# Row sums: a partial sum handed on as an element of the next piece, and SyncE's wait on ScalarE moved into a no-op

## The chip, the cores and the metric

One core of one Trainium2 chip. The metric is the device time of one execution in microseconds. It is some 1.8 us longer than the span that the profile shows (162.37 against 160.6 for the profiled execution of the kernel before).

## The reference

```python
def setup_inputs():
    batch, seq, dim = 32, 512, 1024
    return {"x": np.random.randn(batch, seq, dim).astype(np.float32)}

def reference(x):
    return np.sum(x, axis=-1).astype(np.float32)
```

64 MiB are read, 64 KiB written. There are 16384 rows of 1024 values. Each of the 128 partitions gets 112 rows of a first block and 16 rows of a last one.

## The kernel before

The first seven large tiles are loaded through three buffers and summed by VectorE; ScalarE helps with the seventh. The last tile comes in ever smaller loads: 9, 4 and 2 rows, then the last row in two pieces of 544 and 480 columns. A row that comes late is summed by a custom instruction of VectorE, which adds one half of its columns to the other half and accumulates. Its accumulator can start from a constant or from a value per partition (`scalar`).

```python
    def pairs_dve(xt, a, b, first, acc, pairs):
        h = (a + b) // 2
        nc.vector.tensor_tensor_reduce(
            out=pairs[:, 0 : h - a], in0=xt[:, a:h], in1=xt[:, h:b], scale=1.0, scalar=first,
            op0=ADD, op1=ADD, accum_out=acc,
        )
# ... (the large tiles)
    last = 15 * D
    for i, k in ((0, CUT), (CUT, D)):          # CUT = 544
        nc.sync.dma_start(
            out=xt[:, last + i : last + k],
            in_=x_b[:, c * D + last + i : c * D + last + k],
        )
# ... (rows 0 to 12 of the last 16)
    pairs_dve(xt, 13 * D, 14 * D, 0.0, res[:, c + 13 : c + 14], pairs[2])
    rows_act(xt, res, 14, 1, c + 14)           # ScalarE
    pairs_dve(xt, last, last + CUT, 0.0, part, pairs[0])
    nc.vector.tensor_copy(out=seen, in_=part)
    pairs_dve(xt, last + CUT, last + D, part, res[:, c + 15 : c + 16], pairs[1])
    nc.sync.dma_start(out=out_b, in_=res)      # the store of the last block
```

The copy to `seen` has no use for its value. It carries VectorE's wait for `part`, so that the last sum itself has to wait for its load alone.

## Time and profile before

| | before |
|---|---|
| time, median of the first three runs | 162.13 us (162.09 to 162.22) |
| span of the profiled execution | 160.6 us |
| last load's landing to the end of the span | 2.79 us |
| last custom sum | 467 ns for 240 columns |
| VectorE's end to the start of the store | 64 ns |

The landing is the time at which the last of a transfer's sixteen semaphore updates arrives. The lines themselves stand in the prediction below. In a timeline line the two numbers are start and duration in us; then come engine (SPq is SyncE's queue), source line, operation, and output and input tiles with their sizes. In a group line the number before the last bar is the mean duration of one instruction in ns.

### The profile page before, as it was taken

What the parts mean: (1) busy time and instruction counts of PE and PEld (TensorE: products, weight loads), DVE (VectorE), ACT (ScalarE), POOL (GpSimd) and SP (SyncE); (2) the same over time, 40 slices, a digit from 0 to 9 for tenths busy, and PEclk for the clock granted to TensorE, in tenths of its full rate; (3) what the DMA queues carried; (4) which work ended last, traced back from release to release, by engine and by line L of the source; (5) the groups of instructions that cost most, each with busy time, mean ns of one, the idle gap of its engine ahead of it and who ended that gap; (6) DMA issues with size and microseconds to landing.
All of it is one profiled execution on the core that took longest, in us unless ns stands there. A gap on an engine that the chain in (4) does not pass through costs nothing.

```text
span 160.6 us, 120 instructions
## 1 busy us (share of the span) xinstructions
DVE 121.4 (76%) x16; ACT 17.2 (11%) x31; POOL 0.2 (0%) x4
## 2 busy tenths in 40 slices
DVE  0000059997799958999499994999949999598884
ACT  0000000000000000000000000000000000596892
POOL 0000000000000000000000000000000000000000
DMA  9997996996996996996996979979969969998991
GB/s 375 490 398 337 490 522 294 490 522 261 522 506 278 522 506 278 522 506 278 522 506 278 522 326 457 522 310 473 522 294 490 522 261 522 432 432 369 410 402 62
DMA packets 2169, 67.18 MB, mean 418 GB/s; under 512 B 505, under 2 KB 633, under 8 KB 889
## 3 DMA queue, kind: packets, MB, share of 16 engines
q1 hardware_dynamic: 2016, 67.12, 97.2%
q10 hardware_dynamic: 153, 0.06, 0.1%
HBM read 67.11 MB, written 0.07 MB: 418 GB/s over the span
## 4 chain that ended last, share of the span: by engine, by line
DMA 75%; DVE 22%; SPq 0%; issue 0%; DVEq 0%
DMA xt<-in_x_dram 75%; DVE res L43 21%; DVE pairs L59 1%; SPq L97 0%; DVE seen L114 0%; DVE part L59 0%; DVEq L122 0%; DVE res L59 0%
## 5 line engine op out<-in xcount | busy, mean ns | idle before, releaser
L43 DVE TENSOR_REDUCE res<-xt 128x16 f32<-128x16384 f32 (+3 forms) x9 | 119.8, 13309 | 36.6 <-DMA xt<-in_x_dram 36.6
L51 ACT ACT_TABLE_LOAD x1 | 1.3, 1283 | 138.3 <-DMA xt<-in_x_dram 138.3
L51 ACT ACTIVATE xt<-xt 128x1024 f32<-128x1024 f32 x15 | 15.6, 1042 | 2.2 <-DMA xt<-in_x_dram 2.2
L51 ACT ACTIVATION_READ_ACCUMULATOR xt<-xt 128x1 f32 x15 | 2.8, 186 | 0.0
L59 DVE CUSTOM_DVE_ANT_0 pairs<-xt 128x512 f32<-128x512 f32 (+1 forms) x2 | 1.1, 566 | 0.3 <-DMA xt<-in_x_dram 0.3
L59 DVE CUSTOM_DVE_ANT_0 pairs<-xt,part 128x240 f32<-128x240 f32 x1 | 0.5, 467 | 0.0
L114 DVE COPY seen<-part 128x1 f32<-128x1 f32 x1 | 0.2, 153 | 0.0
L59 DVE DVE_READ_ACCUMULATOR2_ANT res<- 128x1 f32 x2 | 0.2, 81 | 0.0
L159 POOL MEMSET const-bfloat16-1.0<- 128x1 bf16 x1 | 0.1, 101 | 0.0
L159 POOL MEMSET const-uint8-127<- 128x1 uint8 x1 | 0.1, 101 | 0.0
L159 POOL MEMSET const-float32-0.0<- 128x1 f32 x1 | 0.1, 98 | 0.2 <-issue 0.2
L159 POOL MEMSET const-float32-1.0<- 128x1 f32 x1 | 0.1, 98 | 0.0
L59 DVE DVE_READ_ACCUMULATOR2_ANT part<- 128x1 f32 x1 | 0.1, 84 | 0.0
## 6 DMA issues: line engine op xcount, KB each, us to landing
xt<-in_x_dram SPq DMA_DIRECT2D x1, 7680.0 KB
xt<-in_x_dram SPq DMA_DIRECT2D x1, 4608.0 KB, 32.4
xt<-in_x_dram SPq DMA_DIRECT2D x1, 2048.0 KB, 36.9
xt<-in_x_dram SPq DMA_DIRECT2D x1, 1024.0 KB, 39.0
xt<-in_x_dram SPq DMA_DIRECT2D x1, 512.0 KB, 3.9
xt<-in_x_dram SPq DMA_DIRECT2D x1, 272.0 KB, 39.1
xt<-in_x_dram SPq DMA_DIRECT2D x1, 240.0 KB, 38.9
xt<-in_x_dram SPq DMA_DIRECT2D x6, 40.9
```

The costliest lines, as they stand in the source:

```text
L43: nc.vector.tensor_reduce(out=res[:, c : c + n], in_=xt[:, j * D : (j + n) * D].rearrange("p (j d) -> p j d", d=D), axis=X, op=ADD,)
L51: nc.scalar.activation(out=v, in_=v, func=COPY, accum_out=acc)
L59: nc.vector.tensor_tensor_reduce(out=pairs[:, 0 : h - a], in0=xt[:, a:h], in1=xt[:, h:b], scale=1.0, scalar=first, op0=ADD, op1=ADD, accum ...
L114: nc.vector.tensor_copy(out=seen, in_=part)
L159: nc = _bacc.Bacc("TRN2", target_bir_lowering=False, num_devices=1)
```

## The change

Its intent is to shorten what stands behind the last load. The sum of the first piece is written into the column just ahead of the second piece's columns, with a zero beside it. The last sum then takes it as an element and needs no operand per partition. And SyncE's wait for ScalarE, which is over early, goes into a no-op, so that the store's own instruction is left with the wait for VectorE, which is over last.

```diff
-    part = rpool.tile([P, 1], F32, name="part")
-    seen = rpool.tile([P, 1], F32, name="seen")
+    tail = rpool.tile([P, D + 16], F32, name="tail")
+    part = tail[:, CUT + 14 : CUT + 15]
+    nc.vector.memset(tail[:, CUT + 15 : CUT + 16], 0.0)
+    seen = rpool.tile([P, 2], F32, name="seen")
 ... (ScalarE's instructions are kept in the list by_act; pairs_dve loses its argument `first`)
-    for i, k in ((0, CUT), (CUT, D)):
+    for i, k, gap in ((0, CUT, 0), (CUT, D, 16)):
         nc.sync.dma_start(
-            out=xt[:, last + i : last + k],
+            out=tail[:, i + gap : k + gap],
 ...
-    pairs_dve(xt, last, last + CUT, 0.0, part, pairs[0])
+    pairs_dve(tail, 0, CUT, part, pairs[0])
-    nc.vector.tensor_copy(out=seen, in_=part)
-    pairs_dve(xt, last + CUT, last + D, part, res[:, c + 15 : c + 16], pairs[1])
-    nc.sync.dma_start(out=out_b, in_=res)
+    nc.vector.tensor_copy(out=seen, in_=tail[:, CUT + 14 : CUT + 16])
+    pairs_dve(tail, CUT + 14, D + 16, res[:, c + 15 : c + 16], pairs[1])
+    tc.keep_in_program_order(nc.sync.keepalive_nop([nc.sync.lower_ap(res[:, c + 14 : c + 15])]))
+    store = nc.sync.dma_start(out=out_b, in_=res)
+    for i in by_act:
+        tc.declare_no_dep(store.ins, i.ins, reason="the wait is in the nop before it")
```

More of the change, by code (lines that the diff above doesn't have):

```diff
@@ L50, in sum_act, with pairs_dve @@
     def sum_act(v, acc):
-        nc.scalar.activation(out=v, in_=v, func=COPY, accum_out=acc)
+        return nc.scalar.activation(out=v, in_=v, func=COPY, accum_out=acc)
+    by_act = []
     def rows_act(xt, res, j, n, c):
         for i in range(n):
-            sum_act(xt[:, (j + i) * D : (j + i + 1) * D], res[:, c + i : c + i + 1])
-    def pairs_dve(xt, a, b, first, acc, pairs):
+            by_act.append(
+                sum_act(xt[:, (j + i) * D : (j + i + 1) * D], res[:, c + i : c + i + 1])
+            )
+    def pairs_dve(v, a, b, acc, pairs):
         h = (a + b) // 2
         nc.vector.tensor_tensor_reduce(
-            out=pairs[:, 0 : h - a], in0=xt[:, a:h], in1=xt[:, h:b], scale=1.0, scalar=first,
+            out=pairs[:, 0 : h - a], in0=v[:, a:h], in1=v[:, h:b], scale=1.0, scalar=0.0,
             op0=ADD, op1=ADD, accum_out=acc,
@@ L98, in row_sums @@
     last = 15 * D
-    for i, k in ((0, CUT), (CUT, D)):
+    for i, k, gap in ((0, CUT, 0), (CUT, D, 16)):
         nc.sync.dma_start(
-            out=xt[:, last + i : last + k],
+            out=tail[:, i + gap : k + gap],
             in_=x_b[:, c * D + last + i : c * D + last + k],
         )
+    by_act.clear()
     for i, k in zip(cuts[:2], cuts[1:3]):
@@ L108, in row_sums @@
         rows_act(xt, res, i + h, k - i - h, c + i + h)
-    pairs_dve(xt, 13 * D, 14 * D, 0.0, res[:, c + 13 : c + 14], pairs[2])
+    pairs_dve(xt, 13 * D, 14 * D, res[:, c + 13 : c + 14], pairs[2])
     rows_act(xt, res, 14, 1, c + 14)
-    pairs_dve(xt, last, last + CUT, 0.0, part, pairs[0])
-    nc.vector.tensor_copy(out=seen, in_=part)
-    pairs_dve(xt, last + CUT, last + D, part, res[:, c + 15 : c + 16], pairs[1])
-    nc.sync.dma_start(out=out_b, in_=res)
+    pairs_dve(tail, 0, CUT, part, pairs[0])
[5 more added lines that the diff above has]
+        tc.declare_no_dep(store.ins, i.ins, reason="the wait is in the nop before it")
 def kernel(tc: tile.TileContext, x: bass.AP, out: bass.AP):
```

## The prediction

> **What bounds the kernel now.** I read the page first, for what kind of limit there is. The row of DMA shares and the chain that ended last say that almost the whole span is the input stream:
>
> ```profile
> span 160.6 us, 120 instructions
> DMA  9997996996996996996996979979969969998991
> ## 4 chain that ended last, share of the span: by engine, by line
> DMA 75%; DVE 22%; SPq 0%; issue 0%; DVEq 0%
> HBM read 67.11 MB, written 0.07 MB: 418 GB/s over the span
> ```
>
> The stream is not touched by the change, so the question is only what stands between the last load and the end. For that I read the timeline of the last microseconds, then the waits and durations by source line.
>
> Timeline of the kernel before, last part (start, duration, engine, line, operation, output and input):
>
> ```profile
> 156.62 0.69 DVE L59 CUSTOM_DVE_ANT_0 pairs<-xt 128x512 f32<-128x512 f32 x1 [0.26 <-DMA xt<-in_x_dram]
> ...
> 157.24 0.44 DVE L59 CUSTOM_DVE_ANT_0 pairs<-xt 128x272 f32<-128x272 f32 x1
> 157.59 0.19 ACT L51 ACTIVATION_READ_ACCUMULATOR xt<-xt 128x1 f32 x1
> 157.61 0.08 DVE L59 DVE_READ_ACCUMULATOR2_ANT part<- 128x1 f32 x1
> 157.73 0.15 DVE L114 COPY seen<-part 128x1 f32<-128x1 f32 x1
> 157.82 0.47 DVE L59 CUSTOM_DVE_ANT_0 pairs<-xt,part 128x240 f32<-128x240 f32 x1
> 158.22 0.08 DVE L59 DVE_READ_ACCUMULATOR2_ANT res<- 128x1 f32 x1
> 158.36 0.35 SPq L116 DMA_DIRECT2D out_dram<-res  x1
> ```
>
> The reader should see two things. ScalarE's last sum ends at 157.59 + 0.19 = 157.78, half a microsecond before VectorE's at 158.22 + 0.08 = 158.30, so VectorE releases the store. And the last custom sum, with 240 columns, takes 0.47 us, longer than the 0.44 us of the one with 272 columns.
>
> The groups kept apart by shape give these durations to the nanosecond (the number before the last bar):
>
> ```profile
> L59 DVE CUSTOM_DVE_ANT_0 pairs<-xt 128x512 f32<-128x512 f32 x1 | 0.7, 692 | 0.3 <-DMA xt<-in_x_dram 0.3
> L59 DVE CUSTOM_DVE_ANT_0 pairs<-xt,part 128x240 f32<-128x240 f32 x1 | 0.5, 467 | 0.0
> L59 DVE CUSTOM_DVE_ANT_0 pairs<-xt 128x272 f32<-128x272 f32 x1 | 0.4, 441 | 0.0
> L114 DVE COPY seen<-part 128x1 f32<-128x1 f32 x1 | 0.2, 153 | 0.0
> ```
>
> The source lines of the two pieces' loads and of the store show when the last load lands, and a wait on SyncE that stands alone in front of the store:
>
> ```profile
> L100 SPq DMA_DIRECT2D xt<-in_x_dram x2: 328/382/437, 118.1 to 118.9; - x2
> ...
> DMA to landing us min/median/max: 38.9/39.0/39.1
> ...
> L116 SPq EVENT_SEMAPHORE  x1: 20068/20068/20068, 138.3 to 138.3; - x1
> L116 SPq DMA_DIRECT2D out_dram<-res x1: 347/347/347, 158.4 to 158.4; - x1
> ```
>
> The last load is issued at 118.9 and lands 38.9 us later, near 157.8: exactly where the last custom sum starts (157.82). So two things end together there: the copy, and the landing of the last piece. Everything after 157.82 is serial: custom sum, accumulator read, SyncE's wait, store, its landing 1.4 us later, closing barrier.
>
> To price the separate wait I looked at a transfer whose own instruction holds the wait on VectorE, the reload of a large tile:
>
> ```profile
> 99.55 17.22 DVE L43 TENSOR_REDUCE res<-xt 128x16 f32<-128x16384 f32 x1 [2.24 <-DMA xt<-in_x_dram]
> 116.80 0.33 SPq L97 DMA_DIRECT2D xt<-in_x_dram  x1
> ```
>
> VectorE ends at 116.77 and the transfer starts at 116.80, 0.03 us later. The store starts 158.36 - 158.30 = 0.06 us after VectorE.
>
> **What the Trainium skill says.** "VectorE: DVE Perf Modes", section "The TRN2 errata", gives (N+151)/0.96 ns for an fp32 add of two tensors. That is 691 for N = 512 and 441 for 272; this trace has 692 and 441 for the custom sums, so the formula carries over. For 240 it gives 407, and the trace has 467. The section "Scalar operands" of the same page describes the [P, 1] operand read per partition and names no cost for it; the trace's 60 ns is what I take.
>
> The same page, section "The DRAIN you can't avoid", says that a value just written is not safe to read by the next VectorE instruction without a semaphore or one instruction between. That is why the copy to `seen` remains in both kernels: no saving there. This case's traces can't show the hazard itself.
>
> "Perfetto Trace Analysis", section "Identifying Dependency Chains", says that an instruction waiting on several engines may get EventSemaphore instructions ahead of it with the additional conditions. The trace agrees: the 20.07 us EVENT_SEMAPHORE of the store's line is that instruction.
>
> **The change part by part.**
>
> 1. The pointer operand goes. The last custom sum of before starts from `part` as a per-partition scalar. After, `part` and a zero stand in the two columns ahead of the second piece; 482 columns are summed as two halves of 241. Duration by the formula: (241+151)/0.96 = 408 ns; by the slope of the two groups, (692-441)/(512-272) = 1.046 ns per column, 441 - 31 x 1.046 = 409. Take 408. Saving: 467 - 408 = 59 ns. The extra column costs about 1 of these. It lies wholly on the path, since the sum starts with the landing and nothing runs beside it that ends later. One caution: the pointer's cost could stand ahead of the recorded start. But the first 512-column sum too starts with its load's landing, and has no pointer; the landing of the last piece and the start of the sum stand equally close. So I put the cost inside the 467.
>
> 2. The order of waits on SyncE changes. The built program of before has an EventSemaphore that waits for VectorE (and an old transfer), then the store, which itself waits for ScalarE. ScalarE has long been done, so VectorE's end must first release the EventSemaphore, and only then is the store taken up: 0.06 us. After, an EventSemaphore for ScalarE comes first (the no-op), then one for the old transfer, and the store itself waits for VectorE. ScalarE's end at 157.78 leaves half a microsecond for the two, while the ones in a row at the end of the trace take 17 to 28 ns each. The store should then start 0.03 us after VectorE, as the reload does. From the timeline's rounding the saving is 0.06 - 0.03 = 0.03 us; the duration of the wait (from 138.27, 20.068 us, thus to 158.334, and the store about 0.03 later) puts it at 35 ns. Take 35.
>
> 3. A memset of one column is added on VectorE at the start. VectorE is idle until 22.08 us there: 0.
>
> 4. The copy reads two columns instead of one: 1 ns at most, hidden or nearly so behind the landing of the last piece.
>
> 5. The two last loads go to a tile of their own, with a 64-byte gap between them. Same sizes, same order, same queue, the same single wait: 0.
>
> 6. At the very end SyncE waits for the no-op's own semaphore as well as the others. The built program has as many EventSemaphores there as before: 0.
>
> Sum: 59 + 35 = 94 ns, at most 1 or 2 ns given back. 162.13 - 0.094 = 162.04 us.
>
> **The rivals.**
>
> The landing hides it. If the sum's start were what the change made earlier, the last load would eat the gain; the tie at 157.8 says so. But both savings are after that start, so the tie protects nothing. It would matter only for item 4. Had I overlooked something and all were hidden: 162.13.
>
> The read through the stream costs as much as through the pointer. The sum now takes an element that was written some 0.2 us earlier, by an accumulator read; a stall of the stream would show as 441 or more instead of 408. Nothing in the trace shows such a stall: `seen`, the copy that reads `part` directly behind its writer, takes only 153 ns. Then only the 35 ns would stay: 162.10.
>
> The no-op gets in the way: were SyncE to take each EventSemaphore late, after VectorE's end, two would stand in the path instead of one, and the store would start about 0.09 us after VectorE rather than 0.03: 162.13 - 0.06 + 0.03 = 162.10. Against it: half a microsecond between the two engines' ends.
>
> The pieces' new addresses change the landing. It is the one thing that could move the time by more than a tenth, in either direction, as the landing sets the start of the last sum. Against it: same packets, and the three runs of before lie within 0.13 us, which bounds what the stream does from run to run. I allow it 0.1 us.
>
> **Range and chances.** The center is 162.04. The runs of before spread by 0.13 us (162.09 to 162.22), so a median of a few has perhaps 0.04 of its own; the rivals with half the gain stand at 162.10, the one with none at 162.13. I take 161.92 to 162.16 for 8 in 10. Two per cent would be 3.2 us, more than everything behind the last landing (160.6 - 157.8 = 2.8 us in the profile), so "within 2%" is next to certain: 0.99, and 0.005 for each of the others.
>
> **What would show it.** Right: the last custom sum, 241 columns, with about 408 ns; the store's start 0.03 us after the end of VectorE's last accumulator read; the two EVENT_SEMAPHOREs of SyncE over before VectorE ends; from the start of the last sum to the end of the span 94 ns less than the 160.6 - 157.82 = 2.77 us of before. Item 1 is wrong if that sum takes 440 or more; item 2 if the store's gap stays at 0.06. If both are right and the time is still 162.13 or more, the landing of the last load has moved, or the store's 1.4 us has; its row and the last sum's start tell which. The prediction is wrong as a whole if the time leaves the range with the landing where it was.

## The result, and the profile after

| | before | after |
|---|---|---|
| time, median of six runs | 162.13 us (162.09 to 162.22) | 162.13 us (161.97 to 162.25) |
| span of the profiled execution | 160.6 us | 160.4 us |
| last load's landing to the end of the span | 2.79 us | 2.71 us |

The ratio is 0.9999, with a 95% interval of 0.9986 to 1.0012. A ratio here is the mean time of one kernel's runs over that of the other's of the same rounds, so it is not quite the ratio of the medians quoted. The interval is 0.26% wide, some 0.4 us: it can hold the predicted 0.09 us as well as nothing.

The chain of the page is as before:

```profile
span 160.4 us, 122 instructions
DMA 75%; DVE 22%; SPq 0%; issue 0%; DVEq 0%
```

The timeline's end, in the changed kernel:

```profile
157.48 0.19 ACT L55 ACTIVATION_READ_ACCUMULATOR xt<-xt 128x1 f32 x1
157.52 0.08 DVE L67 DVE_READ_ACCUMULATOR2_ANT tail<- 128x1 f32 x1
157.63 0.17 DVE L123 COPY seen<-tail 128x2 f32<-128x2 f32 x1
157.74 0.41 DVE L67 CUSTOM_DVE_ANT_0 pairs<-tail 128x241 f32<-128x241 f32 x1
158.07 0.08 DVE L67 DVE_READ_ACCUMULATOR2_ANT res<- 128x1 f32 x1
158.18 0.35 SPq L128 DMA_DIRECT2D out_dram<-res  x1
```

The groups of its custom sums and of the copy, by shape:

```profile
L67 DVE CUSTOM_DVE_ANT_0 pairs<-tail 128x272 f32<-128x272 f32 x1 | 0.4, 441 | 0.0
L67 DVE CUSTOM_DVE_ANT_0 pairs<-tail 128x241 f32<-128x241 f32 x1 | 0.4, 411 | 0.0
L123 DVE COPY seen<-tail 128x2 f32<-128x2 f32 x1 | 0.2, 168 | 0.0
```

And SyncE's two waits ahead of the store, the no-op's line first (columns: line, engine, operation, count, then shortest/median/longest duration in ns and the first and last start):

```profile
L127 SPq EVENT_SEMAPHORE  x1: 17/17/17, 157.7 to 157.7; - x1
L128 SPq EVENT_SEMAPHORE  x1: 17/17/17, 157.8 to 157.8; - x1
```

So the mechanism stands in the trace as forecast. The last sum has gone from 467 to 411 ns with one column more. Both waits of SyncE are over at 157.8, and the store starts at 158.18, some 0.03 us after VectorE's end at 158.07 + 0.08 = 158.15, where it was 0.06. The copy has gone from 153 to 168 ns.

And yet the medians are equal. Is the time that the trace shows saved behind the last load really saved in the time, and did the scatter of six runs hide it? Or does something give it back ahead of that?

### The profile page after: what moved, and what is told of

It reads as the page before. It is cut to its first block, busy times and chain, and to the rows that moved or that the text cites. A ratio compares the mean times of both kernels' runs of the same rounds, so it can differ in the third digit from the quotient of the medians.

```text
span 160.4 us, 122 instructions
## 1 busy us (share of the span) xinstructions
DVE 121.4 (76%) x17; ACT 17.2 (11%) x31; POOL 0.2 (0%) x4
## 4 chain that ended last, share of the span: by engine, by line
DMA 75%; DVE 22%; SPq 0%; issue 0%; DVEq 0%
DMA xt<-in_x_dram 75%; DVE res L47 21%; DVE pairs L67 1%; SPq L105 0%; DVE seen L123 0%; DVE tail L67 0%; DVEq L136 0%; DVE res L67 0%
## 5 line engine op out<-in xcount | busy, mean ns | idle before, releaser
L67 DVE CUSTOM_DVE_ANT_0 pairs<-xt 128x512 f32<-128x512 f32 x1 | 0.7, 692 | 0.3 <-DMA xt<-in_x_dram 0.3
L67 DVE CUSTOM_DVE_ANT_0 pairs<-tail 128x272 f32<-128x272 f32 (+1 forms) x2 | 0.9, 426 | 0.0
```

What stands on the lines that cost most here:

```text
L67: nc.vector.tensor_tensor_reduce(out=pairs[:, 0 : h - a], in0=v[:, a:h], in1=v[:, h:b], scale=1.0, scalar=0.0, op0=ADD, op1=ADD, accum_out ...
```

## The experiments

Theory A: both savings are real and serial, behind the last landing; the scatter of the stream hides them. Theory B: the new tile (its place in memory, or the memset) makes the last load land later and takes the gain back. Theory C, from the last group of runs on: something else ahead of the last sum gives it back. Three groups of four kernels ran, each group on one chip with the kernel before in its rounds (nine runs of it per group). All results were correct.

### One part alone, both, and none

**The element alone.** The changed kernel, with the store's waits as before:

```diff
-    tc.keep_in_program_order(nc.sync.keepalive_nop([...]))
-    store = nc.sync.dma_start(out=out_b, in_=res)
-    for i in by_act:
-        tc.declare_no_dep(store.ins, i.ins, ...)
+    nc.sync.dma_start(out=out_b, in_=res)
```

> Only the first part of the change: the sum of the first piece as an element, the store's waits in the order of before. Theory A (both savings are real and stand behind the last landing; the run-to-run scatter of the landing hides them in the time): the last custom sum takes 411 ns as in the changed kernel, the store starts 64 ns after VectorE's end as in before; from the last sum's start to the end of the span 2.71 us instead of 2.77; time 0.06 us under before, with an interval wide enough to hold 1. Theory B (the tile of its own or the memset makes the last load land later, and that takes the gain back): the tail is 2.71 us too, but the time is that of before or above, in this run and in the one with both parts, and below it in the run with the no-op alone.

Measured: median 162.24 us (162.01 to 162.65), before 162.27; ratio 1.0002 (0.9989 to 1.0015). Its timeline's end:

```profile
157.72 0.17 DVE L123 COPY seen<-tail 128x2 f32<-128x2 f32 x1
157.79 0.41 DVE L67 CUSTOM_DVE_ANT_0 pairs<-tail 128x241 f32<-128x241 f32 x1
158.12 0.08 DVE L67 DVE_READ_ACCUMULATOR2_ANT res<- 128x1 f32 x1
158.27 0.35 SPq L127 DMA_DIRECT2D out_dram<-res  x1
```

The sum is short (405 ns, not 411), and the store's gap is that of before, 63 ns. From the last sum's start to the end of the span it is 2.70 us.

**The no-op alone.** The kernel before, with the last lines of the change (no-op, store without the dependency on ScalarE) and nothing else:

```diff
-    nc.sync.dma_start(out=out_b, in_=res)
+    tc.keep_in_program_order(nc.sync.keepalive_nop([...res[:, c + 14 : c + 15]...]))
+    store = nc.sync.dma_start(out=out_b, in_=res)
+    for i in by_act:
+        tc.declare_no_dep(store.ins, i.ins, reason="the wait is in the nop before it")
```

> Only the second part: the pointer operand stays, the wait for ScalarE stands in a no-op. Theory A: the last sum takes 467 ns, the store starts 28 ns after VectorE's end, from the last sum's start to the end of the span 2.73 us; time 0.04 us under before. Theory B: time under before by 0.04 us, while the runs with the tile of its own are not.

Measured: median 162.19 us (162.03 to 162.47), ratio 0.9998 (0.9984 to 1.0011).

```profile
157.89 0.15 DVE L119 COPY seen<-part 128x1 f32<-128x1 f32 x1
157.96 0.46 DVE L63 CUSTOM_DVE_ANT_0 pairs<-xt,part 128x240 f32<-128x240 f32 x1
158.34 0.08 DVE L63 DVE_READ_ACCUMULATOR2_ANT res<- 128x1 f32 x1
158.45 0.35 SPq L122 DMA_DIRECT2D out_dram<-res  x1
```

The gap is 28 ns, the sum long (457 ns, not 467), 2.73 us from its start to the end. Each part does its own share and not the other's.

**Both, and none.** The changed kernel again, and the kernel before run against itself; no edit.

> The changed kernel again, in five rounds. Theory A: 411 ns, 28 ns, 2.69 us from the last sum's start to the end; time 0.08 to 0.09 us under before in the mean of more runs, ratio about 0.9995. Theory B: ratio 1.000 again, with the last landing later in the trace than in the runs without the tile of its own.

> The kernel before against itself: what a difference of nothing looks like. Both theories: 467 ns, 64 ns, 2.77 us; ratio 1.000. The distance of the ratio from 1 and the spread of its runs say how small a difference these rounds can show; from the earlier runs I expect a mean within 0.05 us and single runs over 0.15 us.

Measured: both 162.23 us (162.00 to 162.44), ratio 1.0000 (0.9987 to 1.0012); none 162.21 us (162.12 to 162.27), ratio 0.9998 (0.9986 to 1.0011). From the last sum's start to the end: 2.68 and 2.75 us. The times alone don't decide between A and B: the ratios 1.0002, 0.9998 and 1.0000 of the element, the no-op and both are what theory B expected as well, and the 0.06 and 0.08 to 0.09 us that theory A expected of the element and of both is in neither, though each interval holds it. The comparison with itself tells how little these rounds can show: a ratio of 0.9998 out of nothing, as large as what the no-op could bring. Theory B's expectation that the last landing of the run with both parts lies behind the others is not met; it is the earliest of the four (157.55 us, against 157.64 for none, 157.76 for the element alone, 157.90 for the no-op alone).

These traces also correct the picture of the start of the last sum. In the two traces of the prediction and the result, it started 24 and 23 ns after the last landing. In the four of this group it started 30 to 130 ns after it, and 70 to 79 ns after the start of the copy each time. So it often waits for VectorE's own chain (the sum of 272 columns, the copy), and the last load is there already. In that case a sum with the pointer takes 457 ns instead of 467, and one without 404 or 405 instead of 411; why, no run here shows.

### The parts multiplied

To see whether the time follows at all, the disputed costs were multiplied until they stood clear of the scatter.

**Sixteen more sums, with pointer, constant or element.** The first two are made from the kernel before, the third from the changed kernel; each of the sixteen waits for the one before it, the first for the copy or its load. They read the same pointer or element again and again, so only the first reads one that was just written.

```diff
+    junk = rpool.tile([P, 16], F32, name="junk")
 ...
+    for i in range(16):
+        pairs_dve(xt, last + CUT, last + D, part, junk[:, i : i + 1], pairs[1])   # pointer
+        # or: ... last + D, 0.0, junk[...] ...                                    # constant
+        # or: pairs_dve(tail, CUT + 14, D + 16, junk[:, i : i + 1], pairs[1])      # element
```

> The kernel before with 16 more sums of the second piece ahead of the last one, each with the pointer operand, each behind the one before it. Theory A (time follows what stands behind the last landing, and a pointer operand costs 53 to 56 ns): about 467 ns each; time over that of the run with a constant in its place by 16 x 0.055 = 0.9 us. Rival (the pointer's cost shows in the record only of a sum that waits for a load, or time doesn't follow): the two runs differ by less than 0.3 us.

> The same 16 more sums with the constant 0.0 instead of the pointer; the last one keeps its pointer. Theory A: about 409 ns each, 0.44 us from start to start with the waits between, so about 7 us over before, and 0.9 us under the run with pointers. Rival: as the run with pointers within 0.3 us.

> The changed kernel with 16 more sums of 241 columns with the element, each behind the one before it; the element's form multiplied as the pointer's was (8.63 us over before) and the constant's (7.58). Theory A (the element costs its column and nothing else, and the time follows): 408 to 411 ns each, 0.45 us from start to start; time over before by 7.58 + 16 x 0.001 - 0.076 for the changed tail = 7.5 us. Rival (an element just written stalls the stream, or the time does not follow the saving): 8 us or more over before.

Five runs of the pointer and four each of the other two are on record:

| | median us | ratio to before (95%) | start to start, ns |
|---|---|---|---|
| pointer | 170.81 (170.62 to 171.01) | 1.0530 (1.0516 to 1.0544) | 512 |
| constant | 169.79 (169.76 to 169.79) | 1.0467 (1.0453 to 1.0481) | 450 |
| element | 169.83 (169.76 to 169.96) | 1.0467 (1.0453 to 1.0481) | 453 |

The groups of the three kernels, in the order of the table (17 sums with the pointer and 17 with the element, as the kernel's own last sum is of the same kind):

```profile
L60 DVE CUSTOM_DVE_ANT_0 pairs<-xt,part 128x240 f32<-128x240 f32 x17 | 8.0, 468 | 0.6
```

```profile
L60 DVE CUSTOM_DVE_ANT_0 pairs<-xt 128x240 f32<-128x240 f32 x16 | 6.5, 408 | 0.5
```

```profile
L68 DVE CUSTOM_DVE_ANT_0 pairs<-tail 128x241 f32<-128x241 f32 x17 | 7.0, 412 | 0.6
```

Between pointer and constant, which ran on the same chip in the same rounds, the means differ by 170.83 - 169.78 = 1.05 us; the trace has 16 x 62 ns = 0.99. So the pointer costs about 60 ns behind another sum too, and this difference shows in the time. The first of the sixteen, which starts behind the copy, takes 457 ns with the pointer and 405 with the element, the later ones 469 and 411 to 414: the shorter durations belong to a start behind the copy. The element costs next to nothing over the constant: 3 ns from start to start, the same ratio. That an element just written does not stall the stream is shown by the single last sums of the changed kernel (404 to 411 ns), not by this run, whose element was written once.

All three runs took some 0.4 us more than their spans grew: time less span is 2.2 us in them and 1.8 us in all others. No run here says why. It is alike in the three, so it drops out of their differences, but it is in the constant's 7.58 us over before, of which about 7 were expected.

**Ten no-ops behind VectorE's end**, in the kernel before:

```diff
+    for i in range(10):
+        tc.keep_in_program_order(nc.sync.keepalive_nop([nc.sync.lower_ap(res[:, c + 15 : c + 16])]))
     nc.sync.dma_start(out=out_b, in_=res)
```

> The kernel before with ten no-ops on SyncE ahead of the store, all behind VectorE's end. Theory A (an instruction of SyncE's that stands between VectorE's end and the store costs its 60 ns or so, as the row of waits at the end of the trace has it, and the time follows): the store starts 0.6 to 0.7 us after VectorE's end, time 0.5 to 0.6 us over before. Rival (SyncE's waiting instructions pass in no time, or their cost is hidden): the gap stays under 0.2 us and the time is that of before.

Measured: 162.93 us (162.77 to 163.08), ratio 1.0044 (1.0031 to 1.0056), which is 0.71 us. The no-ops' line, and the end of the timeline:

```profile
L117 SPq EVENT_SEMAPHORE  x10: 17/17/17, 158.1 to 158.7; - x10
```

```profile
157.99 0.08 DVE L59 DVE_READ_ACCUMULATOR2_ANT res<- 128x1 f32 x1
158.81 0.35 SPq L118 DMA_DIRECT2D out_dram<-res  x1
```

The store starts 736 ns after VectorE's end instead of 64: ten no-ops cost 672 ns, 67 each, though each is recorded with 17. That is a little over what was expected of both theory and time; the mechanism holds, and so does what the change rests on: an instruction of SyncE's costs time where it stands behind what ends last. Ahead of it the change's two waits cost none (the gap of 28 ns above).

### The tile of its own alone

The kernel before with the last row's pieces in a tile of their own; `part` stays a pointer, the waits as before.

```diff
+    tail = rpool.tile([P, D + 16], F32, name="tail")
 ...
-            out=xt[:, last + i : last + k],
+            out=tail[:, i + gap : k + gap],        # gap: 0 and 16
-    pairs_dve(xt, last, last + CUT, 0.0, part, pairs[0])
+    pairs_dve(tail, 0, CUT, 0.0, part, pairs[0])
-    pairs_dve(xt, last + CUT, last + D, part, res[:, c + 15 : c + 16], pairs[1])
+    pairs_dve(tail, CUT + 16, D + 16, part, res[:, c + 15 : c + 16], pairs[1])
```

> The kernel before with the last row's pieces in a tile of their own with the gap of 64 bytes, nothing else: pointer, order of waits as before. Theory A: the trace of before (467 or 457 ns, 64 ns), ratio 1.000, scatter as in the other runs. Theory B (the tile's place makes the last load land later, and gives back what the change gains): ratio 1.0004 or more, and a last landing behind that of before.

Measured: 162.26 us (162.13 to 162.28), before 162.16; ratio 1.0001 (0.9989 to 1.0014). The last landing lies at 157.61 us, not behind that of before.

```profile
157.65 0.15 DVE L115 COPY seen<-part 128x1 f32<-128x1 f32 x1
157.72 0.46 DVE L60 CUSTOM_DVE_ANT_0 pairs<-tail,part 128x240 f32<-128x240 f32 x1
```

The tail is that of before. Nothing here speaks for theory B; but an interval of 0.2 us on either side doesn't exclude 0.07 us. Over all fourteen traces the last load lands at 157.63 us in the mean of the eight kernels with the tile of its own, and at 157.69 in the mean of the six without; single ones lie from 157.48 to 157.90. That is no sign of a later landing either, though with this scatter it can't exclude 0.07 us.

### The copy of one column, and two more repeats

The changed kernel with its copy cut back to the one column that was just written; the zero beside it is some 150 us old.

```diff
-    seen = rpool.tile([P, 2], F32, name="seen")
+    seen = rpool.tile([P, 1], F32, name="seen")
-    nc.vector.tensor_copy(out=seen, in_=tail[:, CUT + 14 : CUT + 16])
+    nc.vector.tensor_copy(out=seen, in_=part)
```

> The changed kernel with the copy to seen cut back to one column, as in the kernel before. Theory A: the copy takes 153 ns instead of 168; if the last sum waits for VectorE's own chain and not for the last load, it starts 70 ns after the copy instead of 77 to 79, so 8 ns earlier; the time can't show that. Rival (the 15 ns come from the copy's source lying beside the loads, not from its second column): 168 ns again.

Measured: 162.11 us (162.07 to 162.12), before 162.28; ratio 0.9990 (0.9977 to 1.0003).

```profile
L123 DVE COPY seen<-tail 128x1 f32<-128x1 f32 x1 | 0.2, 153 | 0.0
```

The copy is back at 153 ns, so the second column was what cost 15. The last sum starts 71 ns after the copy's start instead of 77 to 78 in the two repeats of its group: 6 to 7 ns. The interval of the time holds 1, so this isn't shown to beat the kernel before, though all five runs (162.07 to 162.12) lie under all nine of before (162.19 to 162.37). The means of the two repeats beside it are 0.07 and 0.10 us higher, far more than those 7 ns: that is not explained by the trace.

The two repeats, with no edit:

> The changed kernel a third time, for the mean of its time. Theory A: 2.68 to 2.69 us from the last sum's start to the end, and with the other repeats a mean 0.07 us under before. Theory C (something ahead of the last sum gives the gain back, which no trace so far shows): a mean within 0.02 us of before again, over all repeats together.

> The changed kernel a fourth time, the same file: as g3. The two together with the runs so far give some 20 runs of the changed kernel; at a scatter of 0.1 to 0.17 us of one run, the mean is good to 0.03 us, which should just tell 0.07 us from nothing.

Measured: 162.09 us (162.05 to 162.41) and 162.19 us (162.11 to 162.37), before 162.28; both ratios 0.9996, with intervals from 0.9982 and 0.9984 to 1.0009.

## Why the prediction was right, and where its sizes were off

The time, 162.13 us, lies inside 161.92 to 162.16, and "within 2%" was right. That alone is no evidence for the mechanism: the range also held the rivals with half of the gain (162.10) and with none (162.13), and the median fell on the latter. The center, 162.04, was not met by the first six runs, so each term of the sum was looked at in ns in ten traces (the ones whose tail is not multiplied). "Store to landing" is to the last of the store's semaphore updates, "to the end" from there on.

| | last sum | VectorE's end to store | store to landing | to the end | last sum's start to the end |
|---|---|---|---|---|---|
| before | 467 | 64 | 1415 | 813 | 2767 |
| before, repeat | 457 | 63 | 1412 | 813 | 2754 |
| tile alone | 457 | 64 | 1418 | 814 | 2761 |
| element alone | 405 | 63 | 1415 | 813 | 2703 |
| no-op alone | 457 | 28 | 1414 | 823 | 2731 |
| after | 411 | 28 | 1421 | 823 | 2691 |
| after, three repeats | 404 to 406 | 27 to 28 | 1414 to 1419 | 822 to 823 | 2676 to 2681 |
| copy of one column | 403 | 27 | 1416 | 823 | 2675 |

- **Item 1, the pointer (59 ns).** Right in kind, a little large: 467 - 411 = 56 ns where the last load releases the sum, 457 - 404 = 53 where VectorE's chain does; 62 from start to start in the multiplied run. That the cost stands inside the recorded duration was right: the sum starts 24 ns after the landing with the pointer and 23 without. The rival of a stall on the element fell: 411 ns, where it asked for 441 or more.
- **Item 2, the waits (35 ns).** 64 - 28 = 36. The no-op and the second wait were over well before VectorE's end; the rival in which two waits get in the way fell. One reading was wrong without harm: the prediction took the 17 to 28 ns recorded for such a wait as its cost, but the four in a row at the end of the trace of before start 58 to 64 ns apart, and the no-op and the wait behind it 84 ns. Both were over 0.36 us before VectorE's end.
- **Item 4, the copy (1 ns at most).** Mis-sized: the second column costs 15 ns. Hidden where the last load sets the sum's start, as the prediction assumed; where VectorE's chain sets it, some 7 ns reach the sum (70 to 71 ns from the copy's start to the sum's without the second column, 77 to 79 with it). "The sum starts with the landing" was true of the trace that the prediction had, and of only one of the nine others of the table.
- **Item 6, the closing (0).** Mis-sized: each of the kernels with the no-op takes 822 to 823 ns from the store's landing to the end, each of the others 813 to 814. The same instructions run there, but two of GpSimd's take longer. The source line of the closing, before and then after (columns as above, duration in ns):

```profile
L122 POOLq DRAIN  x3: 34/41/70, 1.2 to 160.3; - x3
L122 POOLq EVENT_SEMAPHORE_RANGE_CLEAR  x1: 93/93/93, 160.2 to 160.2; - x1
```

```profile
L136 POOLq DRAIN  x3: 34/41/77, 1.2 to 160.2; - x3
L136 POOLq EVENT_SEMAPHORE_RANGE_CLEAR  x1: 95/95/95, 160.0 to 160.0; - x1
```

  The no-op counts up a semaphore of its own, and the drain ahead of the clearing goes from 70 to 77 ns, the clearing from 93 to 95. With the element alone they are 70 and 93 again, with the no-op alone 77 and 95: it comes with the no-op. That the extra semaphore is the reason is argued, not shown.
- **Items 3 and 5, memset and tile (0).** No cost was seen: the memset stands at 1.3 us, where VectorE is idle, and the tile alone has the tail of before.
- **The scatter (0.04 us for a median).** Mis-sized. The prediction said that if both items are right and the time is still 162.13 or more, the last landing or the store has moved. Both were right and the time was 162.13, but in the traces the landing came 0.09 us earlier (157.71 against 157.80) and the store took 6 ns more. What it left out is that the scatter alone can hide 0.09 us: single runs of the changed kernel differ by 0.28 us in the first six.
- **The sum (94 ns).** In the traces it is 2791 - 2714 = 77 ns from the last landing to the end, where the landing sets the start: 56 + 36 = 92 from the two items, less 10 in the closing and 6 in the store's landing (1415 to 1421, which is within its scatter), and 1 from the sum's start. Where VectorE's chain sets it, it is 71: from the start of the sum of 272 columns to the end, 3303 and 3310 ns without the change, 3230, 3238 and 3238 with it.

And the time? Over all 21 runs of the changed kernel, each against the mean of the kernel before in its own rounds, the mean difference is -0.050 us. The single runs scatter by 0.13 us about it, those of before by 0.05; taken as independent, that gives -0.11 to +0.01 us with 95%. The trace's 0.07 to 0.08 lies inside, and so, barely, does nothing. So theory A is shown for the tail in the traces; that the time follows is shown for the pointer's cost multiplied by sixteen and for ten waiting instructions behind VectorE's end. That the kernel as it stands is faster is not shown: its gain is too small for these runs. Theory C with a small part given back isn't excluded. It would have to lie within the span, as time less span is 1.78 to 1.79 us in each of the ten profiled executions of the table. The equal medians of the first result were no sign that the savings are not there.

Open stays why the scatter differs so much between kernels: the sets of the changed kernel have standard deviations of 0.10 to 0.17 us, those of before 0.04 to 0.07, and the sixteen constants and the copy of one column 0.01 and 0.02. With the element alone and the no-op alone it is 0.24 and 0.19, with the tile alone 0.06, so the tile is not the whole cause. No trace shows it, as there is one trace per kernel and the scatter is between runs.

## What to carry to other kernels

Read the tail behind the last landing instruction by instruction. In this custom sum, a value that one instruction hands to the next was 53 to 59 ns cheaper as an element of its stream than as an operand per partition. And the wait that is over last belongs in the instruction that it releases, with the waits that are over early ahead of it: 36 ns here. Ask of each term whether the timing can show it at all: where a term is smaller than the scatter, compare traces from a common event on, and multiply it until the time has to follow.

## What the Trainium skill lacked or had wrong

- The cost of a [P, 1] operand read per partition by a VectorE instruction. "VectorE: DVE Perf Modes", section "Scalar operands", describes it without one: here 53 to 62 ns on each custom sum that has it (468 against 408 ns in the multiplied runs). The formula of the same page's section "The TRN2 errata", (N+151)/0.96 ns, fitted the sums without it: 408 measured for 240 columns, 407 by the formula.
- What a separate waiting instruction costs. "Perfetto Trace Analysis", section "Identifying Dependency Chains", says that such instructions are inserted, not that it matters which condition stays with the instruction itself: 63 to 64 ns from VectorE's end to the store when VectorE's wait is in the inserted one, 27 to 28 when it is in the store. Each further no-op on that path took 67 ns, and was recorded with 17.
- What the record of a waiting instruction covers. The same page, section "Sequencer-only Instruction (DRAIN, etc)", has the record start when all conditions are met. SyncE's wait for two conditions in the kernel before is recorded with 20,068 ns from 138.27 us on, just after its first condition (a landing at 138.25 us), so it includes the wait for the second. With one condition, as in the no-op, the record has 17 ns and no wait.
- No page that was looked up tells what a no-op with a semaphore of its own adds at a program's end: some 10 ns here, in each kernel with it (that the semaphore is the reason is not shown).
- No page that was looked up tells that a copy's second fp32 column can cost 15 ns (153 to 168), where a column more of the custom sums costs 1.05 ns by their slope here, (692 - 441)/(512 - 272).
